# Operand tiles of a hybrid attention layer placed so that moving and stationary rows lie at equal bytes modulo 512

## The chip, the core and the metric

The kernel runs on one core of one Trainium2 chip. The metric is the device time of one execution in microseconds (us), the median of several executions. A core has a matrix engine (PE, with weight loads shown apart as PEld), a vector engine (DVE), a scalar engine (ACT), a third elementwise engine (POOL), and a queue engine (SP) that issues the DMAs. A matmul here is a pair of instructions: a weight load that puts a block of 128 rows by 128 columns of one operand (the stationary one) into the array, and a matmul that streams the rows of the other operand (the moving one) through it. Both operands are read from on-chip memory, where each of the 128 partitions holds a row of bytes; "lies at byte b modulo 512" below always means the start of an operand within such a row.

## What is computed

One decoder layer on 16 meta tokens and 1024 input tokens, 1024 wide. Cut to what matters:

```
a    = rmsnorm(concat(meta, x), ln_mix_pre)
proj = a @ w_in                                  # 3584 columns
y    = concat(diff_attention(proj), hgrn2(proj)) # 4 heads of each kind
h    = concat(meta, x) + rmsnorm(y @ w_out, ln_mix_post)
a    = rmsnorm(h, ln_ffn_pre)
u    = causal_conv3(a @ w_up) + conv_b           # 2 x 2816 columns
gate, up = split(u)
out  = h + rmsnorm((gelu(gate) * up) @ w_down, ln_ffn_post)   # meta rows dropped
```

All inputs and the output are float32.

## The kernel before

To keep float32 accuracy, each large product is done in a rounded float32 type: an operand is split into a high part (`hi`, a rounding) and a low part (`lo`, the rest), and a product is the sum of three matmuls, hi by hi, hi by lo and lo by hi. `split` makes the high part on ACT and the low part on DVE or POOL. The matmuls run in four stages, one after the other, on PE in an order that is fixed by hand (PE is the only engine whose order is the program's own; the order on the others is made by a scheduler).

1. **Projections** (to about 507 us, `proj_step`, lines 234 to 238, and line 886). The weights `wh`, `wl` are stationary; the moving rows are the normalised input, transposed, in the tiles `ahi` and `alo`: 8 blocks (index k) of 1040 columns each. Tokens go in three groups, of 272, 384 and 384 columns. Between these matmuls the small ones of the attention heads and of the HGRN heads are placed.
2. **Output projection** (about 507 to 640 us, `out_part`, lines 1012 to 1016). Here blocks of mixed heads (`mp`, in the slots X1, X2 and mp) are stationary and the split rows of `w_out` (`woh`, `wol`, 512 columns) are moving. Each 128-row block k of `w_out` comes by a DMA into a raw tile `wor` (three buffers in turn), then ACT casts `woh` and DVE or POOL makes `wol`. `out_first` uses blocks k = 0, 1, then 2, 3, then 4 to 6 for the first two token blocks, interleaved with the last HGRN head.
3. **Up projection** (about 640 to 1087 us, `unit`, lines 1378 to 1380). Each of 22 column tiles (`ft`) is done by a seven-product scheme (Strassen-Winograd) for two halves of the tokens: half p = 0 with 258 columns and p = 1 with 256. The products are j = 0 to 6, and each is 12 matmuls: 4 blocks k by three. The moving operands `t{p}_j` are split once and stay; the weights `uh`, `ul` change with each product. On PE the order within an `ft` is j = 0 for p = 0, j = 0 for p = 1, j = 1 for p = 0, and so on: 14 runs of 12 matmuls. 21 of the 22 column tiles go this way; the first is done plainly (lines 1359 to 1361).
4. **Down projection** (about 1087 to 1305 us, `mms`, lines 1536 to 1538). Blocks `gh`, `gl` are stationary, the split weights `wh`, `wl` (512 columns) are moving: 7 products by 11 blocks by 4 row blocks by 3, 924 matmuls.

Where a tile lies follows from the pools: they are stacked, and within a pool tiles lie one behind another. Most weights (`wh`, `wl`) are in a pool of their own that starts from the other end of the memory. `m0` is a constant tile of which 46 columns are used.

Of the kernel before, what the change touches and what calls it, by code (L numbers as in the profile page):

```python
# [9 lines left out]
F32 = mybir.dt.float32  # L10
F32R = mybir.dt.float32r
# [6 lines left out]
P = 128  # L18
META = 16
SEQ = 1024  # L20
L = META + SEQ
D = 1024
KD = D // P
# [3 lines left out]
NBLK = 9  # L27
# [4 lines left out]
WN = [258, 256]  # L32
# [53 lines left out]
def layer_kernel(ctx: ExitStack, tc: tile.TileContext, x, meta, table, lbl, gpre, gpost, win,  # L86
# [25 lines left out]
    def const(shape, name, dt=F32):  # L112
        return cp.tile(shape, dt, tag=name, name=name)
# [12 lines left out]
    nlam = const([P, 1], "nlam")  # L126
    cwt = const([P, 2 * NF, 3], "cwt")
    cbt = const([P, 2 * NF], "cbt")
    m0 = const([P, 152], "m0", F32R)[:, :46]
    G.memset(m0.bitcast(F32), 0.0)  # L130
    m0_7 = const([P, 2, 1, 2], "m0_7", F32R)

# [33 lines left out]

    mx_cm, mxp = pool("mix", 1)

    def long_tile(name):
        return mxp.tile([P, 8, WN[0]], F32, tag="X0", name=name).rearrange("p a c -> p (a c)")  # L170

    def parts_tile(name):
        return mxp.tile([P, 2, 384], F32R, tag="ms", name=f"ms{name}", bufs=2)
# [4 lines left out]
            SY.dma_start(msc[b0:b1, :, l, P * k:P * k + P].rearrange("b p c -> p b c"),  # L178
                         m[:, l, off:off + P * n].bitcast(F32).rearrange("p (b c) -> p b c", c=P))

    ws_cm, wsp = pool("wdsums", 6)
    at_cm, atp = pool("at", 1)
    ahi = atp.tile([P, KD, L], F32R, tag="ahi", name="ahi")
    alo = atp.tile([P, KD, L], F32R, tag="alo", name="alo")

    last_load, lows = [], []

# [59 lines left out]
    xts, xss = {}, {}  # L247

    def spare_tile(tag):
        return mxp.tile([P, 8, WN[0]], F32, tag=tag, name=f"{tag}_in").rearrange("p a c -> p (a c)")  # L250

    def load_x(i, where=None):
        xts[i] = zp.tile([P, D], F32, tag="xt", name=f"xt{i}", bufs=3) if where is None else where
# [719 lines left out]
            interleave(dense(tiles_a, None, wd_sums), [hgrn_head(t_h)] + carried(), FH, 1500)  # L973

    close(at_cm)
    wo_cm, wop = pool("wo", 7)
    y_cm, yp = pool("y0", 1)
    ml_cm, mlp = pool("mixload", 1)
    y0 = yp.tile([P, NBLK, 512], F32, tag="y0", name="y0")
    ssy = yp.tile([P, NBLK, 4], F32, tag="ssy", name="ssy")  # L980
    gpo0 = yp.tile([P, 512], F32, tag="gpo0", name="gpo0")
# [1 line left out]
    def load_wo(n):  # L983
        res = []
        for k in range(KD):
            raw = wp.tile([P, 512], F32, tag="wr", name=f"wor{n}_{k}", bufs=3)
            last_load.append(SY.dma_start(raw, wout[P * k: P * (k + 1), 512 * n: 512 * (n + 1)]))
            if n == 0 and k < 2:
                hi = wp.tile([P, 512], F32R, tag="wh", name=f"woh{n}_{k}", bufs=4)
                lo = wp.tile([P, 512], F32R, tag="wl", name=f"wol{n}_{k}", bufs=4)  # L990
            elif k < 5 if n == 0 else k > 5:
                hi, lo = (wsp.tile([P, 512], F32R, tag="wd", name=f"wo{x}{n}_{k}") for x in "hl")
            else:
                hi = wop.tile([P, 512], F32R, tag="woh", name=f"woh{n}_{k}")
                lo = wop.tile([P, 512], F32R, tag="wol", name=f"wol{n}_{k}")
            if n == 0:
                split(hi, lo, raw, V if k else G)
            else:
                with tc.issue_after(ends["a"].ins), tc.issue_after(ends["v"].ins):
                    split(hi, lo, raw, V if k % 2 else G, halved[0])  # L1000
            res.append((hi, lo))
        return res

    def tok(i):
        return (2, 14) if i == 0 else (P, start(i))
# [27 lines left out]
    def block_tile(n, i):  # L1033
        tag = SLOTS[n][i - 1]
        if tag == "mp":
            return mlp.tile([P, 2, KD, P], F32R, tag="mp", name=f"mp{n}_{i}")
        t = mxp.tile([P, 8, WN[0]], F32R, tag=tag, name=f"mp{n}_{i}")
        return t.rearrange("p a c -> p (a c)")[:, : 2 * KD * P].rearrange("p (l k t) -> p l k t", l=2, k=KD)

    def block_load(m, i, k0, k1):  # L1040
        SY.dma_start(m[:, :, k0:k1].bitcast(F32).rearrange("p l k t -> p l (k t)"), msc[i][:, :, P * k0:P * k1])
# [6 lines left out]
    def second_load(i):  # L1048
        blocks[i] = block_tile(1, i)
        block_load(blocks[i], i, 0, 4)  # L1050
        block_load(blocks[i], i, 4, 7 if i == 1 else 8)
# [51 lines left out]
    def ps_b(name):  # L1103
        return pp.tile([P, 512], F32, tag="b", name=name)
# [3 lines left out]
    e_cm, ep = pool("early", 1, "right")  # L1108
# [7 lines left out]
    q_cm, qp = pool("p2", 2, "right")  # L1116
# [51 lines left out]

    prep_plain()
    wo = load_wo(1)  # L1170
    m7 = ep.tile([P, 8, 2, P], F32R, tag="e1", name="m7")
    for i in range(1, NBLK):
        SY.dma_start(m7[:, i - 1].bitcast(F32), msc[i][:, :, P * (KD - 1):])
    gpo = qp.tile([P, 512], F32, tag="gpo", name="gpo", bufs=1)
# [5 lines left out]
    xhs = {}  # L1180

    def load_xh(i):
        r = tok(i)[0]
        if i:
            xhs[i] = qp.tile([P, D], F32, tag="xh", name=f"xh{i}")
        else:
            both = ep.tile([P, 2 * D], F32, tag="e0", name="xh0")
            xhs[i], xhs["sum"] = both[:, :D], both[:, D:]
        SY.dma_start(xhs[i][:r], meta[14:16, :] if i == 0 else x[P * (i - 1): P * i, :])

    def post(i, py, free=None):
# [47 lines left out]
    tt = [[None] * 8 for _ in range(2)]  # L1239

    def t_tiles(p, j, where, tag):
        if len(tag) == 1:
            both = where.tile([P, 8, WN[p]], F32R, tag=tag[0], name=f"t{p}_{j}")
            return both[:, 0:4], both[:, 4:8]
        both = where.tile([P, 8, int(tag[1])], F32R, tag=tag[0], name=f"t{p}_{j}")
        return both[:, 0:4, : WN[p]], both[:, 4:8, : WN[p]]

    def t_split(p, j, src, where, *tag):
        hi, lo = t_tiles(p, j, where, tag)
        A.copy(hi, src)  # L1250
        V.tensor_tensor(lo, src, hi.bitcast(F32), op=ALU.subtract)
        tt[p][j] = (hi, lo)

    def quarter(p, j):
        n = WN[p]
        a, c = {0: (0, 0), 7: (0, n), 4: (4, 0), 6: (4, n)}[j]
        return at2[p][:, a:a + 4, c:c + n]

    def t_sums(p, where, last):
        b11, b12, b21, b22 = (quarter(p, j) for j in (0, 7, 4, 6))  # L1260
        V.tensor_tensor(b11, b12, b11, op=ALU.subtract)
        V.tensor_tensor(b12, b22, b12, op=ALU.subtract)
        V.tensor_tensor(b22, b22, b11, op=ALU.subtract)
        t_split(p, 1, b22, where, f"t{p}_1")
        t_split(p, 2, b11, where, f"t{p}_2")
        t_split(p, 3, b12, where, f"t{p}_3")
        V.tensor_tensor(b21, b21, b22, op=ALU.subtract)
        t_split(p, 5, b21, *last)

    def run(*args):  # L1270
        for _ in out_part(*args):
            pass

    def k7(i):
        return m7[:, i - 1:i].rearrange("p b l t -> p l b t")

    for i in range(1, NBLK):
        py = ps_b(f"py1_{i}")
        if i >= 3:
            y0_gain(i)  # L1280
        if i == 1:
            load_xh(1)
            load_xh(0)
        if i + 1 < NBLK:
            second_load(i + 1)
            load_xh(i + 1)
        run(blocks[i], py, wo, range(4), True, False)
        if i == 3:
            trans(1)
        run(blocks[i], py, wo, range(4, 7 if i == 1 else 8), False, i > 1)  # L1290
        if i > 3:
            trans(i - 2)
        if i == 5:
            trans(0)
        if i == 1:
            pm = ps_b("py1_0")
            for _ in meta_part(pm, wo, True):
                pass
# [12 lines left out]
        if i == 2:  # L1311
            post(0, ysum[:, :512], ysum[:, 512:])
        if i == 5:
            t_split(0, 0, quarter(0, 0), ep, "e0")
            t_split(0, 4, quarter(0, 4), ep, "e1")
        if i == 7:
            t_split(0, 7, quarter(0, 7), mxp, "X2", WN[0])
            t_split(0, 6, quarter(0, 6), mxp, "X1", WN[0])
        if i in (2, 3):
            for p in (1 + 2 * i, 2 + 2 * i):  # L1320
                out_last(p)
    close(q_cm, ml_cm, y_cm, wo_cm, ws_cm)

    xu_cm, xup = pool("xu", 2)
    t_cm, tp = pool("tsplit", 1)

    marks = {}

# [85 lines left out]
        next(p0)  # L1414
    trans(8)
    t_split(1, 7, quarter(1, 7), tp, "t1_5")
    t_split(1, 6, quarter(1, 6), mxp, "X0", WN[0])
    t_sums(0, tp, (mxp, "X2", WN[0]))
    close(a_cms.pop())
    t2_cm, t2p = pool("tsplit2", 1)  # L1420
    p1 = plain_unit(1, ps_b)
    for j in range(4):
        prep(7 + j)
        next(p1)
    t_sums(1, t2p, (tp, "t1_5"))
    close(a_cms.pop(), b_cm)
    v_cm, cv = pool("conv", 2, "right")
    dn_cm, dn = pool("down", 4, "right")
    next(p0)
    for j in range(4, 7):  # L1430
# [257 lines left out]
```

## Time and profile before

| what | value |
|---|---|
| median of three runs | 1307.29 us (1307.03 to 1307.64) |
| the profiled execution's own time | 1307.29 us |
| its span, first to last instruction | 1305.5 us |
| mean granted PE clock | 0.998 |
| PE busy in the span | 1277.2 us (98%) |
| PE busy, 644 to 1087 us | 439.41 of 443.00 us |
| PE busy, 1087 to 1305.5 us | 208.95 of 218.50 us |

Reading aids: an instruction's duration for PE overlaps that of the next one, since matmuls are pipelined, so the pace of a stage is read from start to start, not from the mean duration. In the timeline a row has start and duration in us, engine, line, operation, tiles (written<-read), shape and how many equal ones were merged. In the table of stretches a row has the stretch, its length, and for each engine its busy time and its count of instructions.

### The profile page before, as it was taken

How to read it: one execution, taken by the hardware profiler on the slowest of the kernel's cores; microseconds unless marked ns; L12 is line 12 of the kernel's file. 1: busy time of each engine (PE TensorE's matmuls, PEld its weight loads, DVE VectorE, ACT ScalarE, POOL GpSimd, SP SyncE). 2: the span in 40 equal slices, each digit the busy share in tenths (PEclk: the TensorE clock that was granted, in tenths of full speed). 3: DMA queues.
4: the chain of work that ended last, by engine and by line, in shares of the span. 5: the costliest groups of instructions: out<-in, count | busy, mean ns of one | idle time of the engine just before them, and what ended most of it. 6: DMA issues, size and time to landing. Idle time of an engine off the chain costs nothing.

```text
span 1305.5 us, 26100 instructions
## 1 busy us (share of the span) xinstructions
PE 1277.2 (98%) x10154; PEld 1182.0 (91%) x10154; DVE 884.8 (68%) x1488; ACT 696.5 (53%) x1639; POOL 482.9 (37%) x387
## 2 busy tenths in 40 slices
PE   8999999999999999999999999999999999999997
PEld 7999999899999998767999999999999997888875
DVE  7574647465645574548997877877877767697586
ACT  8565466546644763447754444544544544454553
POOL 5231423242323310352076666566576631010121
PEclk9999999999999999999999999999999999999999
DMA  5243655183643533687222222222222137955263
GB/s 214 94 100 87 125 116 114 57 157 79 116 128 69 122 109 109 224 270 261 91 75 89 82 74 73 90 75 81 90 74 81 57 122 268 318 188 168 82 210 121
DMA packets 116418, 165.04 MB, mean 126 GB/s; under 512 B 10099, under 2 KB 57523, under 8 KB 116294
## 3 DMA queue, kind: packets, MB, share of 16 engines
q1 hardware_dynamic: 93062, 151.84, 35.6%
q0 software_dynamic: 23232, 11.54, 7.5%
q8 instruction: 80, 1.31, 0.4%
q14 instruction: 44, 0.36, 0.1%
HBM read 134.24 MB, written 52.17 MB: 143 GB/s over the span
## 4 chain that ended last, share of the span: by engine, by line
PE 81%; DVE 6%; DMA 4%; ACT 4%; issue 2%; SPq 0%; POOL 0%; DVEq 0%; ACTq 0%; POOLq 0%
PE pd L1537 5%; PE pd L1536 5%; PE pd L1538 5%; PE pb L1378 4%; PE pb L1380 4%; PE pb L1379 4%; PE pa L1378 3%; PE pa L1380 3%; PE pa L1379 3%; PE pc L1378 3%; PE pc L1379 3%; PE pc L1380 3%; PE pa L732 3%; PE pi_hf L234 1%; DMA ra<-in_wup_dram 1%
## 5 line engine op out<-in xcount | busy, mean ns | idle before, releaser
L1378 PE MATMUL pb<-t,uh 128*128 128x258 f32 x504 | 142.3, 282 | 2.5 <-DVE u L53 2.5
L1379 PE MATMUL pb<-t,uh 128*128 128x258 f32 x504 | 141.6, 281 | 0.0
L1380 PE MATMUL pb<-t,ul 128*128 128x258 f32 x504 | 141.6, 281 | 0.0
L1537 PE MATMUL pd<-wl,gh 128*128 128x512 f32 x308 | 122.0, 396 | 1.1 <-DVE wl L53 1.1
L1536 PE MATMUL pd<-wh,gh 128*128 128x512 f32 x308 | 121.8, 395 | 0.1
L1538 PE MATMUL pd<-wh,gl 128*128 128x512 f32 x308 | 121.7, 395 | 0.0
L53 DVE SCALAR_TENSOR_TENSOR c<-uu,cwt,c 128x514 f32<-128x514 f32 (+1 forms) x88 | 97.2, 1104 | 19.6 <-ACT c L53 18.9
L53 POOL TENSOR_TENSOR c<-c,c 128x514 f32<-128x514 f32 (+1 forms) x44 | 63.8, 1449 | 122.4 <-ACT c L53 120.4
L1378 PEld LDWEIGHTS pb<-t,uh 128*128 128x128 f32 x504 | 95.5, 189 | 3.0 <-DVE u L53 2.9
L1379 PEld LDWEIGHTS pb<-t,uh 128*128 128x128 f32 x504 | 95.5, 189 | 0.0
L1378 PE MATMUL pa<-t,uh 128*128 128x258 f32 (+1 forms) x336 | 95.2, 283 | 0.0
L1380 PEld LDWEIGHTS pb<-t,ul 128*128 128x128 f32 x504 | 95.2, 189 | 0.0
L1380 PE MATMUL pa<-t,ul 128*128 128x258 f32 (+1 forms) x336 | 95.1, 283 | 0.0
L1379 PE MATMUL pa<-t,uh 128*128 128x258 f32 (+1 forms) x336 | 94.8, 282 | 0.0
L1378 PE MATMUL pc<-t,uh 128*128 128x258 f32 (+1 forms) x336 | 94.4, 281 | 0.0
L1379 PE MATMUL pc<-t,uh 128*128 128x258 f32 (+1 forms) x336 | 94.0, 280 | 0.0
L1380 PE MATMUL pc<-t,ul 128*128 128x258 f32 (+1 forms) x336 | 93.7, 279 | 0.0
L53 DVE SCALAR_TENSOR_TENSOR c<-ug,cwt,c 128x514 f32<-128x514 f32 (+1 forms) x88 | 88.3, 1005 | 1.4 <-ACT c L53 0.6
L53 ACT CAST uh<-ra 128x512 fp32r<-128x512 f32 x67 | 41.1, 616 | 62.2 <-PE pb L1379 41.1
L53 POOL TENSOR_TENSOR ul<-ws,uh 128x512 fp32r<-128x512 f32 x42 | 60.5, 1440 | 35.5 <-ACT uh L53 34.8
L1537 PEld LDWEIGHTS pd<-wl,gh 128*128 128x128 f32 x308 | 57.7, 187 | 16.4 <-DVE wl L53 2.6
L53 DVE TENSOR_TENSOR ul<-ra,uh 128x512 fp32r<-128x512 f32 x42 | 38.7, 921 | 49.4 <-ACT uh L53 49.4
(388 smaller groups left out, 4166.3 us busy)
## 6 DMA issues: line engine op xcount, KB each, us to landing
ra<-in_wup_dram SPq DMA_DIRECT2D x88, 256.0 KB, 2.7
mp<-msc SPq DMA_DIRECT2D x23, 512.0 KB, 5.0
tsc<-in_wdown_dram SPq DMA_DIRECT2D x44, 256.0 KB, 4.8
wi<-tsc SPq DMA_DIRECT2D x44, 256.0 KB, 2.8
gi<-gsc SPq DMA_DIRECT2D x33, 256.0 KB, 5.3
wi<-in_wdown_dram SPq DMA_DIRECT2D x33, 256.0 KB, 5.3
gsc<-c SPq DMA_DIRECT2D x22, 257.0 KB, 2.1
tsc<-in_wdown_dram POOLq DMA_DIRECT2D x22, 256.0 KB, 7.5
```

The lines of the kernel that those rows point to most:

```text
L53: ins = call(*args, **kw)
L234: T.matmul(pt, hi[:, s], ahi[:, k, t0:t1], start=(k == 0), stop=False)
L732: T.matmul(po[:, :P], w_, vn[:, j], start=(j == 0), stop=(j == i))
L1378: T.matmul(pt, hi[:, s], th[:, k], start=(first and k == 0), stop=False, skip_group_check=True)
L1379: T.matmul(pt, hi[:, s], tl[:, k], start=False, stop=False, skip_group_check=True)
L1380: T.matmul(pt, lo[:, s], th[:, k], start=False, stop=(k == 3), skip_group_check=True)
L1536: T.matmul(py, gh[:, s], wh, start=(k == 0 and pr not in (3, 7)), stop=False, skip_group_check=True)
L1537: T.matmul(py, gh[:, s], wl, start=False, stop=False, skip_group_check=True)
L1538: T.matmul(py, gl[:, s], wh, start=False, stop=(k == NH - 1), skip_group_check=True)
```

## The change

No instruction is added. Tiles are made larger, shifted or put in another order, so that for most matmuls the moving and the stationary operand start at equal bytes modulo 512. The distance (start of the moving rows less start of the next stationary rows, modulo 512 bytes), as the two programs lay them out:

| matmuls | count | distance before | distance in the change |
|---|---|---|---|
| projections, group of 272 columns | 672 | 0, 64, ... 448, one step with each k | 448 |
| projections, groups of 384 | 1344 | 0, 64, ... 448, one step with each k | 0 |
| output projection, 512 columns | 418 | mostly 192, 128 and 352, few at 64 and 256 | 0 for 366 |
| up, p = 0 (258 columns), j = 0 to 6 | 252 each | 448, 256, 320, 384, 384, 320, 256 | 384, 0, 0, 0, 448, 0, 0 |
| up, p = 1 (256 columns), j = 0 to 6 | 252 each | 256, 448, 448, 448, 256, 256, 384 | 0 for all |
| down, 512 columns | 924 | 288 | 0 |

For p = 0 the number is that of the first block; each further block adds 8, and the low part lies 32 further (in the change not for j = 3). The same holds for p = 1, j = 6 before, by its tile's row length. For the up stage and the projections the stationary rows stay where they were, at 480, and the moving ones move; in the down stage the stationary ones move.

The pool `wdsums` of six tiles, which take the split blocks k = 2 to 4 of the first half of `w_out`, was opened ahead of the pool `at` of `ahi` and `alo`; it is now opened as `wosplit` after `at` is closed, in the memory that `ahi` and `alo` leave. That moves work on DVE, ACT and SP.

```
-    m0 = const([P, 152], "m0", F32R)[:, :46]
+    m0 = const([P, 88], "m0", F32R)[:, :46]
...
+    MIX = {"X0": 2048, "X1": 2176, "X2": 2176}
+    def mix_tile(tag, dt, name):
+        return mxp.tile([P, MIX[tag]], dt, tag=tag, name=name)
...
-    ws_cm, wsp = pool("wdsums", 6)
     at_cm, atp = pool("at", 1)
-    ahi = atp.tile([P, KD, L], F32R, tag="ahi", name="ahi")
-    alo = atp.tile([P, KD, L], F32R, tag="alo", name="alo")
+    ahi, alo = (atp.tile([P, KD, P * NBLK], F32R, tag=t, name=t)[:, :, P - META:] for t in ("ahi", "alo"))
...
     close(at_cm)
+    ws_cm, wsp = pool("wosplit", 6)
     wo_cm, wop = pool("wo", 7)
+    ml_cm, mlp = pool("mixload", 1)
     y_cm, yp = pool("y0", 1)
-    ml_cm, mlp = pool("mixload", 1)
...
-    m7 = ep.tile([P, 8, 2, P], F32R, tag="e1", name="m7")
+    xh0 = ep.tile([P, 2 * D], F32, tag="e0", name="xh0")
+    m7 = ep.tile([P, 8 * WN[0]], F32R, tag="e1", name="m7")[:, 16:].rearrange("p (b l t) -> p b l t", b=8, l=2)
...
     def t_tiles(p, j, where, tag):
-        if len(tag) == 1:
-            both = where.tile([P, 8, WN[p]], F32R, tag=tag[0], name=f"t{p}_{j}")
-            return both[:, 0:4], both[:, 4:8]
-        both = where.tile([P, 8, int(tag[1])], F32R, tag=tag[0], name=f"t{p}_{j}")
-        return both[:, 0:4, : WN[p]], both[:, 4:8, : WN[p]]
+        tag, n, lo = (tag + (8 * WN[p], 4 * WN[p])[len(tag) - 1:])[:3]
+        flat = where.tile([P, n], F32R, tag=tag, name=f"t{p}_{j}")
+        return [flat[:, o:o + 4 * WN[p]].rearrange("p (a c) -> p a c", a=4) for o in (0, lo)]
...
-        t_split(p, 1, b22, where, f"t{p}_1")
-        t_split(p, 2, b11, where, f"t{p}_2")
-        t_split(p, 3, b12, where, f"t{p}_3")
+        for j, b in ((1, b22), (2, b11), (3, b12)):
+            t_split(p, j, b, where, f"t{p}_{j}", *(() if p else (2304, 1152) if j == 3 else (2176,)))
...
     t_cm, tp = pool("tsplit", 1)
+    tp.tile([P, 48], F32, tag="gap", name="gap")
...
     v_cm, cv = pool("conv", 2, "right")
+    cv.tile([P, 56], F32, tag="gap2", name="gap2", bufs=1)
```

On PE the order of instructions is the same. It differs on DVE, ACT and SP where the projections end and the output projection begins. DVE before, from the gate of the last HGRN head on (`wol_k` is the low part of block k of `w_out`, `woh_k` its high part, `wor_k` the raw block, `gate` and `hq` belong to the last HGRN head):

```order
L53 TENSOR_TENSOR gate_6154<-pi_hg_1_6161,sg_1_6222 128x384
L53 TENSOR_SCALAR sg_2_6253<-sg_2_6253 128x384
L53 TENSOR_TENSOR wol_5_6311<-wor_5_6308,woh_5_6310 128x512
L53 TENSOR_TENSOR wol_6_6317<-wor_6_6314,woh_6_6316 128x512
L53 TENSOR_TENSOR gate_6154<-pi_hg_2_6228,sg_2_6253 128x384
L53 TENSOR_TENSOR wol_7_6323<-wor_7_6320,woh_7_6322 128x512
L53 TENSOR_TENSOR hq_5424<-hq_5424,f_5421 128x1040
```

And DVE in the change, at the same place:

```order
L53 TENSOR_TENSOR gate_6151<-pi_hg_1_6158,sg_1_6219 128x384
L53 TENSOR_SCALAR sg_2_6250<-sg_2_6250 128x384
L53 TENSOR_TENSOR wol_2_6293<-wor_2_6290,woh_2_6292 128x512
L53 TENSOR_TENSOR wol_3_6299<-wor_3_6296,woh_3_6298 128x512
L53 TENSOR_TENSOR gate_6151<-pi_hg_2_6225,sg_2_6250 128x384
L53 TENSOR_TENSOR wol_4_6305<-wor_4_6302,woh_4_6304 128x512
L53 TENSOR_TENSOR wol_5_6311<-wor_5_6308,woh_5_6310 128x512
L53 TENSOR_TENSOR hq_5421<-hq_5421,f_5418 128x1040
L53 TENSOR_TENSOR wol_6_6317<-wor_6_6314,woh_6_6316 128x512
L53 TENSOR_TENSOR wol_7_6323<-wor_7_6320,woh_7_6322 128x512
```

Blocks 2, 3 and 4, which stood some forty rows earlier, now stand where 5, 6 and 7 did, and 6 and 7 come behind `hq`. SP's queue before, at the loads of these blocks (`msc` is the store of mixed heads, `gpo` a gain row, `mp_3` the third token block of mixed heads):

```order
L987 DMA wor_2_6290<-in_wout_dram 128x512
L987 DMA wor_3_6296<-in_wout_dram 128x512
L987 DMA wor_4_6302<-in_wout_dram 128x512
L987 DMA wor_5_6308<-in_wout_dram 128x512
L178 DMA msc<-msa_5_6037 128x3x128 x2
L987 DMA wor_6_6314<-in_wout_dram 128x512
L987 DMA wor_7_6320<-in_wout_dram 128x512
L1058 DMA gpo_6271<-in_gpost_dram 128x512
L1041 DMA mp_3_6335<-msc 128x2x512
L1041 DMA mp_3_6335<-msc 128x2x384
```

And in the change:

```order
L991 DMA wor_2_6290<-in_wout_dram 128x512
L183 DMA msc<-msa_5_6034 128x3x128 x2
L991 DMA wor_3_6296<-in_wout_dram 128x512
L991 DMA wor_4_6302<-in_wout_dram 128x512
L1061 DMA gpo_6271<-in_gpost_dram 128x512
L1044 DMA mp_3_6335<-msc 128x2x512
L991 DMA wor_5_6308<-in_wout_dram 128x512
L991 DMA wor_6_6314<-in_wout_dram 128x512
L991 DMA wor_7_6320<-in_wout_dram 128x512
L1044 DMA mp_3_6335<-msc 128x2x384
```

The loads of blocks 5 to 7 moved behind the gain row and the first half of `mp_3`; the raw tile that each takes is free when the low part of block 2, 3 or 4 is made.

More of the change, by code (lines that the diff above doesn't have):

```diff
@@ L167, in layer_kernel @@
     mx_cm, mxp = pool("mix", 1)
+    MIX = {"X0": 2048, "X1": 2176, "X2": 2176}
+    def mix_tile(tag, dt, name):
+        return mxp.tile([P, MIX[tag]], dt, tag=tag, name=name)
     def long_tile(name):
-        return mxp.tile([P, 8, WN[0]], F32, tag="X0", name=name).rearrange("p a c -> p (a c)")
+        return mix_tile("X0", F32, name)
     def parts_tile(name):
@@ L249, in spare_tile @@
     def spare_tile(tag):
-        return mxp.tile([P, 8, WN[0]], F32, tag=tag, name=f"{tag}_in").rearrange("p a c -> p (a c)")
+        return mix_tile(tag, F32, f"{tag}_in")
     def load_x(i, where=None):
@@ L1036, in block_tile @@
             return mlp.tile([P, 2, KD, P], F32R, tag="mp", name=f"mp{n}_{i}")
-        t = mxp.tile([P, 8, WN[0]], F32R, tag=tag, name=f"mp{n}_{i}")
-        return t.rearrange("p a c -> p (a c)")[:, : 2 * KD * P].rearrange("p (l k t) -> p l k t", l=2, k=KD)
+        return mix_tile(tag, F32R, f"mp{n}_{i}")[:, : 2 * KD * P].rearrange("p (l k t) -> p l k t", l=2, k=KD)
     def block_load(m, i, k0, k1):
@@ L1186, in load_xh @@
         else:
-            both = ep.tile([P, 2 * D], F32, tag="e0", name="xh0")
-            xhs[i], xhs["sum"] = both[:, :D], both[:, D:]
+            xhs[i], xhs["sum"] = xh0[:, :D], xh0[:, D:]
         SY.dma_start(xhs[i][:r], meta[14:16, :] if i == 0 else x[P * (i - 1): P * i, :])
@@ L1316, in layer_kernel @@
         if i == 7:
-            t_split(0, 7, quarter(0, 7), mxp, "X2", WN[0])
-            t_split(0, 6, quarter(0, 6), mxp, "X1", WN[0])
+            t_split(0, 7, quarter(0, 7), mxp, "X2", MIX["X2"])
+            t_split(0, 6, quarter(0, 6), mxp, "X1", MIX["X1"])
         if i in (2, 3):
@@ L1321, in layer_kernel @@
                 out_last(p)
-    close(q_cm, ml_cm, y_cm, wo_cm, ws_cm)
+    close(q_cm, y_cm, ml_cm, wo_cm, ws_cm)
     xu_cm, xup = pool("xu", 2)
     t_cm, tp = pool("tsplit", 1)
+    tp.tile([P, 48], F32, tag="gap", name="gap")
     marks = {}
@@ L1416, in layer_kernel @@
     t_split(1, 7, quarter(1, 7), tp, "t1_5")
-    t_split(1, 6, quarter(1, 6), mxp, "X0", WN[0])
-    t_sums(0, tp, (mxp, "X2", WN[0]))
+    t_split(1, 6, quarter(1, 6), mxp, "X0")
+    t_sums(0, tp, (mxp, "X2", MIX["X2"]))
     close(a_cms.pop())
```

## The prediction

> **What bounds the kernel now.** I read the page first: the span, each engine's busy time, the chain of waits.
>
> ```profile
> span 1305.5 us, 26100 instructions
> PE 1277.2 (98%) x10154; PEld 1182.0 (91%) x10154; DVE 884.8 (68%) x1488; ACT 696.5 (53%) x1639; POOL 482.9 (37%) x387
> PE 81%; DVE 6%; DMA 4%; ACT 4%; issue 2%; SPq 0%; POOL 0%; DVEq 0%; ACTq 0%; POOLq 0%
> ```
>
> PE is busy for 98% of the span and carries 81% of the chain. Nothing is added to it or taken from it, so the time can move in two ways only: the pace at which the same 10154 matmuls start, and new waits. The profiled execution took 1307.29 us, which is also the median; 1.8 us lie outside its span. I add my terms to 1307.3. What a measurement of this kernel can tell from no change is about 0.2%, 2.6 us: below 1304.7 is faster, above 1309.9 slower.
>
> For the pace I read PE's timeline in the up stage, at the first matmul of each run of twelve. It is one column tile, j = 0 of p = 1 first; rows of p = 1 (256 columns) and p = 0 (258) alternate.
>
> ```profile
> 840.00 0.28 PE L1378 MATMUL pa<-t,uh 128*128 128x256 f32 x1
> 841.44 0.28 PE L1378 MATMUL pb<-t,uh 128*128 128x258 f32 x1
> 842.88 0.28 PE L1378 MATMUL pb<-t,uh 128*128 128x256 f32 x1
> 844.29 0.28 PE L1378 MATMUL pc<-t,uh 128*128 128x258 f32 x1
> 845.71 0.28 PE L1378 MATMUL pc<-t,uh 128*128 128x256 f32 x1
> 847.07 0.29 PE L1378 MATMUL pb<-t,uh 128*128 128x258 f32 x1
> 848.52 0.28 PE L1378 MATMUL pb<-t,uh 128*128 128x256 f32 x1
> 849.90 0.29 PE L1378 MATMUL pa<-t,uh 128*128 128x258 f32 x1
> 851.35 0.28 PE L1378 MATMUL pa<-t,uh 128*128 128x256 f32 x1
> 852.78 0.28 PE L1378 MATMUL pb<-t,uh 128*128 128x258 f32 x1
> 854.20 0.28 PE L1378 MATMUL pb<-t,uh 128*128 128x256 f32 x1
> 855.63 0.28 PE L1378 MATMUL pc<-t,uh 128*128 128x258 f32 x1
> 857.07 0.28 PE L1378 MATMUL pc<-t,uh 128*128 128x256 f32 x1
> 858.50 0.28 PE L1378 MATMUL pa<-t,uh 128*128 128x258 f32 x1
> 859.94 0.28 PE L1378 MATMUL pa<-t,uh 128*128 128x256 f32 x1
> ```
>
> From start to start the seven p = 1 runs take 1.44, 1.41, 1.36, 1.38, 1.43, 1.43, 1.43, together 9.88 us. Beside them I put the distances of the change's table: 256, 448, 448, 448, 256, 256, 384. So twelve equal matmuls cost 1.43 to 1.44 at a distance of 256 and 1.36 to 1.41 at 448. Distance matters, and so does the state in which a run begins, since 448 gives three values. The p = 0 runs, from j = 1 on and j = 0 last, take 1.44, 1.42, 1.45, 1.45, 1.42, 1.44, 1.44, together 10.06, at 256, 320, 384, 384, 320, 256, 448. The column tile lasts 19.94 us.
>
> **What distance 0 is worth.** The up stage never has it. The projections do, where the distance grows by 64 with each block of three matmuls; here are blocks 0, 1, 4, 5 and the end of the eighth step (the timeline, first matmul of each).
>
> ```profile
> 252.70 0.34 PE L234 MATMUL pi_hg<-ahi,wh_hg 128*128 128x384 f32 x1
> 253.23 0.33 PE L234 MATMUL pi_hg<-ahi,wh_hg 128*128 128x384 f32 x1
> ...
> 254.80 0.33 PE L234 MATMUL pi_hg<-ahi,wh_hg 128*128 128x384 f32 x1
> 255.32 0.34 PE L234 MATMUL pi_hg<-ahi,wh_hg 128*128 128x384 f32 x1
> ...
> 256.38 0.34 PE L234 MATMUL pi_hg<-ahi,wh_hg 128*128 128x384 f32 x1
> ```
>
> Three matmuls take 0.53 us at distance 0, 0.52 at 256, and (256.38 - 252.70) / 7 = 0.526 on average. Zero is not better than the rest, and within the 10 ns of the rows it does as 256 does. I take that for the forecast: the pattern repeats after 256 bytes, and equal bytes are the slow case of the up stage.
>
> **Up, +4.1.** In the change all p = 1 runs are at 0. At 1.43 to 1.44 each they take 10.01 to 10.08, which is 0.13 to 0.20 more than 9.88. For p = 0 five runs are at 0 (1.44 each), one at 384 (1.45), one at 448 (1.44): 10.09, 0.03 more. The sum is 0.16 to 0.23 for a column tile, middle 0.195, and 21 of the 22 go this way: 3.4 to 4.8, I take 4.1. The other end is that 0 is the free case that 256 is not. The best run (1.36) stands for it: 7 x 1.36 = 9.52, and 258/256 of it, 9.59, for p = 0. That saves 0.36 + 0.47 = 0.83 a tile, 17 us in all.
>
> **Down, -2.9.** Here the view is the table of stretches.
>
> ```profile
> core 0: us, PE busy (x) PEld busy (x) DVE busy (x) ACT busy (x) POOL busy (x), PEclk, DMA share, GB/s
> 1094.00:1242.00 148.00, 148.00 (x635) 118.75 (x635) 109.66 (x165) 74.45 (x146) 12.84 (x8) 1.00 0.62 206
> ```
>
> PE never idles, at a granted clock of 1.00, so one matmul costs 148 / 635 = 0.2331 us, at distance 288 throughout. The nearest rows for 512 columns at another distance are in the output projection, a change of place within the same loop (timeline again).
>
> ```profile
> 507.26 0.39 PE L1012 MATMUL py<-woh,mp 128*128 128x512 f32 x1
> ...
> 508.39 0.39 PE L1016 MATMUL py<-woh,mp 128*128 128x512 f32 x1
> 508.62 0.40 PE L1012 MATMUL py<-woh,mp 128*128 128x512 f32 x1
> ...
> 511.64 0.39 PE L1014 MATMUL py<-wol,mp 128*128 128x512 f32 x1
> ...
> 552.96 0.39 PE L1012 MATMUL py<-woh,mp 128*128 128x512 f32 x1
> ...
> 553.88 0.39 PE L1014 MATMUL py<-wol,mp 128*128 128x512 f32 x1
> ```
>
> From 507.26 to 508.39 the distance is 256: five steps of 0.226, the fastest pace of this shape. From 508.62 to 511.64 it is 192: thirteen steps of 0.2323. From 552.96 to 553.88 it is 256 again: four steps of 0.230. The same distance gives two paces, as 448 does in the up stage; and short runs need not show the pace that a long one settles at. The bounds are therefore 0.226 (924 x 0.0071 = 6.6 saved) and no gain. I take 0.230, the slower of the two rows: 924 x 0.0031 = 2.9 saved.
>
> **Output projection, -0.8.** 366 matmuls come to 0; from 0.2323 to 0.230 that is 0.8, bounds 0 and 366 x 0.0063 = 2.3.
>
> **Projections, 0.** The groups of 384 columns go from the mean of eight distances to 0, 0.526 against 0.53 by the rows above: within a row's rounding. The best pace of the up stage, 1.36 / 12 for 256 columns, gives 0.170 for 384, so that 1344 x (0.526 / 3 - 0.170) = 7 us could be saved, and about 3 on the 672 of 272 columns at the same excess; on the other side 1344 x 0.004 / 3 = 1.8 could be lost.
>
> **The hand-over, +2.0.** The pool `wosplit` now lies in the memory of `ahi` and `alo`, so the splits of blocks 2 to 4 wait for the last projection matmul (507.1). What that drags along shows in the timeline on PE, ACT, DVE and SP's queue, and in the landing times of the DMA issues of 505 to 520 and of the whole page.
>
> ```profile
> 507.85 0.61 ACT L53 CAST woh<-wor 128x512 fp32r<-128x512 f32 x1
> 508.49 0.69 DVE L53 TENSOR_TENSOR wol<-wor,woh 128x512 fp32r<-128x512 f32 x1
> 509.59 1.03 SPq L987 DMA_DIRECT2D wor<-in_wout_dram  x2
> wor<-in_wout_dram SPq DMA_DIRECT2D x3, 256.0 KB, 5.7
> ra<-in_wup_dram SPq DMA_DIRECT2D x88, 256.0 KB, 2.7
> 512.80 1.24 DVE L53 TENSOR_TENSOR hq<-hq,f 128x1040 f32<-128x1040 f32 x1 [1.50 <-PE pd L436]
> 513.91 0.39 PE L1014 MATMUL py<-wol,mp 128*128 128x512 f32 x1
> 514.61 0.39 PE L1014 MATMUL py<-wol,mp 128*128 128x512 f32 x1
> ```
>
> The raw tiles of blocks 5 to 7 are now those of 2 to 4 and come free with the low parts, on DVE from 507.4 on. Before, the blocks after 4 could be loaded ahead; now the loads stand in SP's queue behind the gain row and the first half of `mp_3`, so they go at about 509.6 at the earliest. They land 2.7 (a load of equal size, whole page) to 5.7 us later (median of the window): 512.3 to 515.3. A cast (0.61) and a low part (0.69) make block 5's low part ready at 513.6 to 516.6, against a use at 513.91. Then DVE does `hq` (1.24) and block 6 (0.69): 515.5 to 518.5, against 514.61. Late are 0.9 to 3.9, and PE has nothing else in its order; queued behind on DVE is block 7, needed 0.7 after block 6 and ready as long after it. I take 2.0. Nothing later hides it, since PE bounds the rest.
>
> The other edits (a smaller `m0`, gaps, `xh0` opened earlier, two pools swapped) issue nothing and only place tiles.
>
> **Sum:** 1307.3 + 4.1 - 2.9 - 0.8 + 0 + 2.0 = 1309.7 us. Its own range, with the hand-over's bounds and up's, is 1307 to 1312.
>
> **Rivals.**
>
> *Long runs settle slow.* The up stage's 1.44 at 256 is a settled excess that stays through twelve matmuls, and down has runs of 924. If 0 holds the excess there too, down and output projection gain nothing: 1307.3 + 4.1 + 2.0 = 1313.4, slower. For it: the pace at 256 is already 0.230 in the second stretch. Against it: 0.226 in the first.
>
> *The pace of 507.26 is the lasting one.* Down saves 6.6 and the output projection 2.3: 1307.3 + 4.1 - 6.6 - 2.3 + 2.0 = 1304.5, at the edge of faster. For it: five steps in succession. Against it: the stretch at 552.96.
>
> *Equal bytes free every stage.* 0 and 256 would differ, and all runs go at their best: 1307.3 - 17.3 - 6.6 - 2.3 - 10 + 2.0 = 1273. Against it: the 0.53 at 252.70, at exactly this distance.
>
> *Placement is worth nothing* and only the hand-over is left: 1307.3 + 2.0 = 1309.3. Against it: 1.36 and 1.44 for equal instructions. The Trainium skill speaks for it ("SBUF — State Buffer", section "Who interferes with whom"): it gives PE two read ports, one for the moving operand and one for the weight load, independent of each other, so that where one lies could not disturb the other. By that rule the sum would lose its first four terms; the trace does not agree, since the runs of the up stage differ by 0.08 us at the same shapes, with PE waiting for no other engine.
>
> **How the numbers follow.** Chances: my sum 33%, slow settling 32%, the fast pace in down 20%, all stages free 8%, placement worth nothing 7%. The range takes in the first three and the last with their bounds, 1302 to 1315, and leaves out the free case and some tails. Faster: the free case, half of the fast pace and a little of the first, 22%. Within 0.2%: half of my sum, most of placement worth nothing, the rest of the fast pace, 30%. Slower: the rest, 48%.
>
> **What would show it.** A column tile of the up stage lasts 20.13 instead of 19.94, with all seven p = 1 runs at 1.43 to 1.44; the same stretch of the down stage holds about 643 matmuls (148 / 0.230) instead of 635, or 655 at 0.226; the triples of the projections stay at 0.53; and between 513 and 519 PE waits about 2 us for `wol` on DVE. The forecast is wrong if the p = 1 runs fall to 1.36 with all at distance 0, if the pace in down rises above 0.2331, or if the loads of blocks 5 to 7 land before 512.

## The result and the profile after

| | before | the change |
|---|---|---|
| median of 14 runs each | 1307.07 us | 1308.16 us (1307.37 to 1313.38) |
| ratio to before, 95% interval | | 1.0014 (1.0004 to 1.0024) |
| the profiled execution's own time | 1307.29 us | 1310.98 us |
| its span | 1305.5 us | 1309.2 us |

The change costs about 0.14%, with an interval that lies just above 1; that is below the 0.2% that the prediction took as the least it could tell from no change. The profiled execution is one of the longer ones, 2.8 us above the median; part of what it has more is told with the hand-over below. Three moves that nearly cancel lie behind the small number. The page of the change first: span, busy time, chain.

```profile
span 1309.2 us, 26099 instructions
PE 1275.9 (97%) x10154; PEld 1186.7 (91%) x10154; DVE 887.3 (68%) x1488; ACT 697.0 (53%) x1639; POOL 480.8 (37%) x387
PE 82%; DVE 6%; ACT 4%; DMA 4%; issue 2%; SPq 0%; POOL 0%; DVEq 0%; ACTq 0%
```

It reads as before: the same 10154 matmuls, PE busy nearly all the time. So I compared the start of the n-th matmul in the two traces, which works because PE's order is the same. The difference after less before, in us, at the ends of the stages:

| up to | difference |
|---|---|
| last matmuls ahead of the first new wait (514 us) | +0.2 |
| behind the new waits (522 us) | +4.3 |
| start of the up stage | +4.5 |
| end of the up stage | +8.4 |
| last matmul | +3.5 |

So the hand-over costs 4.1, the up stage 3.9, and the down stage gives back 4.9. The up stage, on PE's timeline of the change (first matmul of some runs of twelve; `t` is 256 wide in p = 1, 258 in p = 0):

```profile
845.97 0.28 PE L1379 MATMUL pa<-t,uh 128*128 128x256 f32 x1
847.39 0.28 PE L1379 MATMUL pb<-t,uh 128*128 128x258 f32 x1
848.83 0.28 PE L1379 MATMUL pb<-t,uh 128*128 128x256 f32 x1
850.26 0.28 PE L1379 MATMUL pc<-t,uh 128*128 128x258 f32 x1
851.70 0.28 PE L1379 MATMUL pc<-t,uh 128*128 128x256 f32 x1
853.14 0.28 PE L1379 MATMUL pb<-t,uh 128*128 128x258 f32 x1
...
866.11 0.28 PE L1379 MATMUL pa<-t,uh 128*128 128x256 f32 x1
```

The p = 1 run that took 1.36 before (j = 2, from 845.71) takes 853.14 - 851.70 = 1.44 now, and the others 1.42 and 1.43: all stand at the slow value. The column tile lasts 866.11 - 845.97 = 20.14 us. The down stage, in the same stretch as before:

```profile
1094.00:1242.00 148.00, 147.95 (x650) 121.49 (x650) 110.12 (x168) 73.31 (x139) 9.84 (x8) 1.00 0.67 219
```

650 matmuls in place of 635, so 148 / 650 = 0.2277 us each. And the hand-over, on ACT, DVE and SP's queue, then what PE waited for from 513 to 520:

```profile
509.48 2.44 SPq L991 DMA_DIRECT2D wor<-in_wout_dram  x3
508.75 0.69 DVE L53 TENSOR_TENSOR wol<-wor,woh 128x512 fp32r<-128x512 f32 x1
515.76 1.96 ACT L53 CAST woh<-wor 128x512 fp32r<-128x512 f32 x3 [5.05 <-DMA wor<-in_wout_dram]
516.41 0.69 DVE L53 TENSOR_TENSOR wol<-wor,woh 128x512 fp32r<-128x512 f32 x1 [4.85 <-ACT woh L53]
517.02 1.23 DVE L53 TENSOR_TENSOR hq<-hq,f 128x1040 f32<-128x1040 f32 x1
518.17 0.69 DVE L53 TENSOR_TENSOR wol<-wor,woh 128x512 fp32r<-128x512 f32 x1
PE py L1016 <- ACT woh L53: 1.7, 1, 1.7
PE py L1018 <- DVE wol L53: 0.2, 1, 0.2
```

The chain can be followed row by row. DVE makes the low part of block 2 from 508.75 to 509.44; 0.04 later SP issues the load into the raw tile that this frees; ACT's cast of block 5 begins when it lands, at 515.76, 6.3 after the issue; PE waits 1.66 us for that cast. Then come block 5's low part, `hq`, and block 6's low part, which is done at 518.86. The matmul that uses it, before and in the change:

```profile
515.56 0.48 PE L1014 MATMUL py<-wol,mp 128*128 128x512 f32 x1
518.91 0.80 PE L1018 MATMUL py<-wol,mp 128*128 128x512 f32 x1
```

It starts 3.35 us later than before, where the matmuls at 514 us started 0.2 later: the chain costs 3.1 of the 4.1. The other 1.0 comes behind it, under a lower granted clock (stretches of the same trace: length, PE busy and count, granted clock, DMA share, GB/s):

```profile
517.00:518.00 1.00, 0.84 (x3) 0.92 0.04 14
518.00:520.00 2.00, 1.97 (x7) 0.50 0.50 141
520.00:521.00 1.00, 1.00 (x9) 0.50 0.89 272
521.00:522.00 1.00, 1.00 (x67) 0.87 1.01 254
```

By these rows the clock was at one half for some 3.4 us; in the kernel before it is 1.00 from 513 to 520.

### The profile page after: what moved, and what is told of

It reads as the page before. It is cut to its first block, busy times and chain, and to the rows that moved or that the text cites. A ratio compares the mean times of both kernels' runs of the same rounds, so it can differ in the third digit from the quotient of the medians.

```text
span 1309.2 us, 26099 instructions
## 1 busy us (share of the span) xinstructions
PE 1275.9 (97%) x10154; PEld 1186.7 (91%) x10154; DVE 887.3 (68%) x1488; ACT 697.0 (53%) x1639; POOL 480.8 (37%) x387
## 4 chain that ended last, share of the span: by engine, by line
PE 82%; DVE 6%; ACT 4%; DMA 4%; issue 2%; SPq 0%; POOL 0%; DVEq 0%; ACTq 0%
PE pd L1539 5%; PE pd L1540 5%; PE pd L1538 5%; PE pb L1379 5%; PE pb L1380 4%; PE pb L1381 4%; PE pa L735 3%; PE pa L1379 3%; PE pa L1381 3%; PE pa L1380 3%; PE pc L1379 3%; PE pc L1380 3%; PE pc L1381 3%; PE pt L711 1%; PE S L655 1%
## 5 line engine op out<-in xcount | busy, mean ns | idle before, releaser
L53 POOL TENSOR_TENSOR c<-c,c 128x514 f32<-128x514 f32 (+1 forms) x44 | 63.8, 1450 | 122.6 <-ACT c L53 119.2
```

The source lines that it names most:

```text
L53: ins = call(*args, **kw)
```

## The experiments

**The pace by distance, measured alone.**

```diff
+    for n in (512, 256, 258, 272, 384):
+        for r in range(0, 512, 16):
+            a = 120 + r // 4
+            for _ in range(3):
+                py = banks[g % 4][:, :n]
+                g += 1
+                for q in range(12):
+                    T.matmul(py, w, mv[:, a:a + n], start=(q == 0), stop=(q == 11))
```

> This kernel computes nothing of the layer: it writes zeros to the output and runs 5760 matmuls of one shape after another, 36 for each distance from 0 to 496 in steps of 16, at 512, 256, 258, 272 and 384 columns. Theory (the pace is set by the distance modulo 256 and the width): at 256 columns the steps at a distance and at that distance plus 256 agree within 1 ns, 120 at 0 and 256 and 113 to 118 at 192 and 448; at 512 columns 227 at 0 and 233 at 32 (that is 288). Rival (equal bytes modulo 512 are a case of their own): 0 and 256 differ at 512 columns. Second rival (the pace follows from the neighbouring engines' traffic, not from the distance): with the other engines idle all distances run at one pace, 113 at 256 columns and 227 at 512.

Four rows of its timeline (start, time from the first start to the last end, count): 512 columns at distance 0 and 288, 256 columns at 0 and 112.

```profile
7.45 5.83 PE L114 MATMUL b<-mv,st 128*128 128x512 f32 x25
157.63 6.00 PE L114 MATMUL b<-mv,st 128*128 128x512 f32 x25
273.31 3.28 PE L114 MATMUL b<-mv,st 128*128 128x256 f32 x26
303.18 3.11 PE L114 MATMUL b<-mv,st 128*128 128x256 f32 x26
```

One matmul lasts 0.39 or 0.28, so a step is (5.83 - 0.39) / 24 = 0.2267 against (6.00 - 0.39) / 24 = 0.2338, and (3.28 - 0.28) / 25 = 0.120 against (3.11 - 0.28) / 25 = 0.113. PE alone is at work here, so neighbouring traffic is not what makes the difference. All settled paces, in ns, as the mean of the last twelve of 36 steps from the start times in the trace:

| distance mod 256 | 0 | 16 | 32 | 48 | 64 | 80 | 96 | 112 | 128 | 144 | 160 | 176 | 192 | 208 | 224 | 240 |
|---|---|---|---|---|---|---|---|---|---|---|---|---|---|---|---|---|
| 256 columns | 120.0 | 118.8 | 116.7 | 118.3 | 117.8 | 120.0 | 120.0 | 113.3 | 118.8 | 118.3 | 117.1 | 119.4 | 113.3 | 118.7 | 117.9 | 117.4 |
| 258 | 120.0 | 116.7 | 120.0 | 120.0 | 118.6 | 120.2 | 120.0 | 120.0 | 120.0 | 120.0 | 119.7 | 120.0 | 120.8 | 121.7 | 120.3 | 119.2 |
| 272 | 126.7 | 124.6 | 125.7 | 125.0 | 126.7 | 125.0 | 126.7 | 123.3 | 126.7 | 124.4 | 123.3 | 123.3 | 123.3 | 126.7 | 126.7 | 125.0 |
| 384 | 173.3 | 175.5 | 173.3 | 175.0 | 173.3 | 173.3 | 176.7 | 173.3 | 175.8 | 174.7 | 176.7 | 176.4 | 176.7 | 176.7 | 173.3 | 180.0 |
| 512 | 226.7 | 231.7 | 233.3 | 233.3 | 228.9 | 231.1 | 233.3 | 231.1 | 231.7 | 233.3 | 234.2 | 233.3 | 233.3 | 234.8 | 233.3 | 226.7 |

The same distance plus 256 gives the same mean within 0.4 ns at every place of the table. So equal bytes modulo 512 are no case of their own, and what distance is good depends on the width: 0 is among the best for 512 columns and among the worst for 256. At 512 columns and 256 bytes the first twelve steps average 229.9 and the last twelve 226.7. That fits the two paces the prediction found at one distance in the output projection, if its slower row was a short run that had not settled. In this map only the moving rows change place, so by itself it cannot tell the distance from the moving rows' own place. The down stage can: there the stationary rows were moved, and its two paces, 233.3 and 226.9 ns from start to start, are those of the map at 288 and at 0 within 0.2 ns.

**Another distance with the same remainder.**

```diff
-    m0 = const([P, 88], "m0", F32R)[:, :46]
+    m0 = const([P, 152], "m0", F32R)[:, :46]
-    cv.tile([P, 56], F32, tag="gap2", name="gap2", bufs=1)
+    cv.tile([P, 120], F32, tag="gap2", name="gap2", bufs=1)
```

(To make room, `t0_3` is laid out as `t0_1` is, its low part 32 bytes further.)

> The change with moving and stationary rows 256 bytes apart modulo 512 in the projections, the up and the down stage, in place of 0. Theory (the pattern repeats after 256 bytes): no difference, 1308.2 us within 1.5, with a column tile of the up stage at 20.14 us and the down stage at 0.2277 a matmul as in the change. Rival (equal bytes modulo 512 matter as such): the down stage loses its gain of 4 to 5 us, 1312.5 or more.

1309.31 us, ratio to before 1.001 (1.000 to 1.0019), against 1.0014 for the change. From start to end of the up stage it loses 3.9 us on the kernel before, and the down stage gives back 5.1; in the stretch from 1094 to 1242 us it has 651 matmuls. At these distances 256 bytes more make no difference in the kernel either.

**The down stage alone.**

```diff
     v_cm, cv = pool("conv", 2, "right")
+    cv.tile([P, 56], F32, tag="gap2", name="gap2", bufs=1)
```

(on the kernel before)

> The kernel before with the gap in the pool of the down stage alone, which brings that stage from a distance of 288 to 0. Theory: 924 matmuls at 0.2277 in place of 0.2331, 4 to 5 us less, 1302.5 us. Rival (the gain in the trace of the change came from loads that stood earlier, since everything before was later by 8 us): 1306 to 1307.

1302.49 us, ratio 0.9958 (0.9945 to 0.9972), 650 matmuls in the stretch again. One unused tile of 224 bytes, which moves `gh` and `gl` and leaves `wh` and `wl` where they are, is worth 4.8 us by the medians, and the gain needs nothing of the rest of the change.

**The hand-over taken out, and alone.** The first puts the pool back where it was in the change (for which `ahi` and `alo` need their old layout, and X1 and X2 are 2112 long in place of 2176), the second moves it in the kernel before.

```diff
+    ws_cm, wsp = pool("wosplit", 6)
     at_cm, atp = pool("at", 1)
-    ahi, alo = (atp.tile([P, KD, P * NBLK], F32R, tag=t, name=t)[:, :, P - META:] for t in ("ahi", "alo"))
+    ahi, alo = (atp.tile([P, KD, L], F32R, tag=t, name=t) for t in ("ahi", "alo"))
...
     close(at_cm)
-    ws_cm, wsp = pool("wosplit", 6)
```

> The change with the pool of the split blocks opened ahead of ahi and alo again, and so with the projections' old layout. Theory: the wait at the hand-over, about 4 us in the trace, goes and nothing else moves: 1304.2 us, slightly faster than before. Rival: PE would have met the same wait a little later, at a store or load of mixed heads, so that 2 us or less come back: 1306 to 1308.

1306.73 us, ratio 0.9994 (0.9985 to 1.0003). In its trace the wait is gone: from the last projection matmul to the start of the up stage it moves by nothing against the kernel before (0.9 to 0.9 us), then up +3.9 and down -5.4. Against the change it saves 0.2% by the two ratios to before, 2.6 us (1.4 by the bare medians), and I had expected 4, from the one trace with the half clock in it. The time falls in the range that the rival gave, 1306 to 1308, but not for its reason: no such wait comes back later in the trace.

```diff
-    ws_cm, wsp = pool("wdsums", 6)
     at_cm, atp = pool("at", 1)
...
     close(at_cm)
+    ws_cm, wsp = pool("wosplit", 6)
     wo_cm, wop = pool("wo", 7)
```

> The kernel before with the pool of the split blocks opened where ahi and alo are closed, and nothing else: all distances are those of before. Theory (a wait on PE at the hand-over, 2.4 and 4.1 us in two traces, and nothing gives it back): 1307.1 + 2.5 = 1309.6 us, between 1308.8 and 1311. Rival (what the split blocks lose is made good by the memory that opens earlier, or was due to the new layout of ahi and alo): 1307.1 within 0.7.

1310.06 us (1307.45 to 1311.90), ratio 1.0017 (1.0007 to 1.0026): 0.17% of 1307.8, 2.2 us slower. PE's waits in its trace from 513 to 520 us:

```profile
PE py L1012 <- ACT woh L53: 1.2, 1, 1.2
PE py L1014 <- DVE wol L53: 0.7, 2, 0.5
518.00:520.00 2.00, 1.55 (x42) 1.00 0.43 146
```

The same waits on the same blocks, 1.9 us, with the clock at 1.00 (last row): the half clock of the change's profiled execution is not a fixed part of the price. The matmul with block 6's low part is 2.7 us late here, and 2.4 in the trace of the run 256 bytes apart, with the first load landing 5.9 and 5.6 us after its issue. Up to the start of the up stage further waits move this again: against the kernel before, the stretch from the last projection matmul to there is longer by 4.2 us in the change's trace, 3.0 in that of the run 256 bytes apart and 4.3 here. One trace gives the price to about a microsecond; the ratios are the better measure. The distances are all those of the kernel before, so the layout of `ahi` and `alo` has no part in it.

**Can the up stage be had without the loss?** The map offers 112 for 256 columns. A second one ran pairs of runs as the up stage does, to find a partner for p = 0.

```diff
+    def twelve(pt, hi, lo, step, n):
+        for k in range(4):
+            for q, a in enumerate((hi, lo, hi)):
+                o = 120 + (a + k * step) // 4
+                T.matmul(pt[:, :n], w, mv[:, o:o + n], start=(k + q == 0), stop=(k == 3 and q == 2))
...
+                    for _ in range(2):
+                        twelve(banks[g % 4], r0, r0 + lo, step, 258)
+                        twelve(banks[(g + 1) % 4], r1, r1, 0, 256)
+                        g += 2
```

> This kernel computes nothing of the layer: zeros are written to the output, and 8448 matmuls run as the up stage has them, twelve of 258 columns (four blocks of high, low, high) and then twelve of 256, with the 256 ones at a distance of 112 and the 258 ones at distances that start from 0 to 248, with the low part at several offsets, and with 8 or 0 bytes from block to block. Theory (distance, width and the state left by the run before set the pace, and nothing else): every run of 256 columns settles at 113.3 within its twelve, so 1.36 to 1.37 us against 1.433 at distance 0; the 258 ones spread from about 1.39 to 1.46, and the settings that the change has (0 with the low part at 32) give 1.44. Rival (112 was fast only because 96 came before it): the 256 ones stay at 1.40 or more behind most settings.

The rival was right in the main: of 175 settings at 112 that can be timed, the second p = 1 run took under 1.37 us in 11 and 1.38 to 1.43 in 157. A run of twelve does not come to the pace of a long one by itself; which p = 0 run stands before it decides. The best with the up stage's own steps (8 bytes a block, low part at 32) was a start at 8: 1.434 + 1.360 = 2.794 us. It was built into the kernel, with the pool where it was before the change and the gaps set to suit:

```diff
+    AT = {(0, 1): 42, (0, 2): 42, (0, 3): 42, (0, 5): 18, (0, 6): 18, (1, 6): 44, (0, 0): 2, (0, 4): 2, (1, 0): 4, (1, 1): 4, (1, 2): 4, (1, 3): 4, (1, 4): 4, (1, 5): 4}
...
+        n = tag[1] if len(tag) > 1 else 2056 if (p, j) == (1, 3) else 2112
+        flat = where.tile([P, n], F32R, tag=tag[0], name=f"t{p}_{j}")
+        a, w = AT.get((p, j), 0), 4 * WN[p]
+        return [flat[:, o:o + w].rearrange("p (a c) -> p a c", a=4) for o in (a, a + w)]
```

> The kernel with the old pool order at the hand-over (as in pool_back) and with the up stage's tiles at other distances: 112 modulo 256 for all p = 1 runs, 8 rising by 8 with each block (low part 32 further) for all p = 0 runs, down and output projection at 0 as in the change. Theory (the distances alone set the pace, so the pair measured by itself carries over): a pair of runs takes 1.434 + 1.360 = 2.794 us in place of 2.874, a column tile 19.56 in place of 20.14, and 21 of them save 12 us against pool_back: 1306.7 - 12 = 1295 us. Rival (with DVE, ACT and POOL busy beside PE the fast state does not last, as one of three runs at 448 in the kernel before went at 1.415): the p = 1 runs come to 1.39 to 1.41, a column tile to 19.8, and the time to 1299 or more.

1303.65 us, ratio 0.9969 (0.9958 to 0.9979). A pair of its timeline, with the start of the next:

```profile
850.41 0.28 PE L1382 MATMUL pa<-t,uh 128*128 128x258 f32 x1
851.86 0.28 PE L1382 MATMUL pa<-t,uh 128*128 128x256 f32 x1
853.27 0.28 PE L1382 MATMUL pb<-t,uh 128*128 128x258 f32 x1
```

The pair takes 1.45 and 1.41, and does so for all seven j and every column tile from the third on. The pair measured alone did not carry over: same distances, another steady sequence, 2.85 in place of 2.79. That is the number of the rival, but its reason (the busy engines beside PE) was not tested.

**Is it the state, or the weights' places?** One more map laid the weights as the kernel does and passed through the settings upwards and downwards; and one kernel took the pair that the kernel before itself had run fastest, j = 2.

> This kernel computes nothing of the layer: zeros are written to the output, and pairs of runs go as in the up stage, now with weights that lie as there (high, high, low, four blocks), three equal pairs for each start distance of the 258 columns from 0 to 248 (low part 32 further, 8 more with each block), once upwards and once downwards, with the 256 columns at 112 and then at 192. Theory (a setting has more than one lasting state, and the state before chooses): the third pair of some settings differs between the upward and the downward pass, and 8 with 112 gives 2.794 in one and 2.853 in the other. Rival (the weights' places beyond 256 bytes count): both passes give 2.853 at 8 with 112, and agree everywhere.

At 112 both passes agree, and 8 gives 2.794 in both; at 192 some settings settle differently from the two sides (a start at 24: 2.840 upwards, 2.800 downwards). Other settings alternate between two values from pair to pair (a start of 176 with 112: 2.874, 2.812, 2.874). So one setting can have more than one state that holds over the three pairs, which supports the first part of the theory; but the 2.853 of the kernel at 8 with 112 appeared in neither pass. The weights' places, as far as this map copies them, are not it. What in the kernel chooses another state stays open: the maps run with the other engines idle and on zeros, so neither the neighbours nor the data are excluded.

```diff
-    AT = {(0, 1): 42, (0, 2): 42, (0, 3): 42, (0, 5): 18, (0, 6): 18, (1, 6): 44, (0, 0): 2, (0, 4): 2, (1, 0): 4, (1, 1): 4, (1, 2): 4, (1, 3): 4, (1, 4): 4, (1, 5): 4}
+    AT = {(0, 1): 32, (0, 2): 32, (0, 3): 32, (0, 5): 32, (0, 6): 32, (0, 0): 16, (0, 4): 16}
...
-    tp.tile([P, 24], F32, tag="gap", name="gap")
+    tp.tile([P, 48], F32, tag="gap", name="gap")
```

> As the run named best, with all p = 0 runs at 64 (modulo 256, 8 more with each block, low part 32 further) and all p = 1 runs at 192: the pair that took 1.417 + 1.359 = 2.776 as j = 2 in the kernel before. Theory (distances set the pace, state and all): if the state that j = 2 had there lasts, a column tile takes 19.43, 0.50 less than before, and the time is 1303.65 - 21 x (19.97 - 19.43) = 1292.3 us. Rival (the pair falls into another lasting state once it follows itself): a column tile of 19.8 to 20.0 and 1300 to 1304 us.

1298.70 us, ratio 0.9931 (0.9918 to 0.9945): faster than both kernels, 9.3 us below its runs of before by the medians. Its timeline:

```profile
850.12 0.28 PE L1382 MATMUL pb<-t,uh 128*128 128x258 f32 x1
851.55 0.28 PE L1382 MATMUL pb<-t,uh 128*128 128x256 f32 x1
852.91 0.28 PE L1382 MATMUL pc<-t,uh 128*128 128x258 f32 x1
```

The p = 1 run takes 1.36 and stays there in all seven j; the p = 0 run takes 1.43 where 1.417 was hoped for. A column tile lasts 19.55 us, where the theory said 19.43 and the rival 19.8 or more. The pair is 2.793 us here, was 2.776 as j = 2 in the kernel before, and is 2.814 in the last map: three values for one setting. The stage gains 5.4 us on the kernel before, not 21 x 0.38 = 8.0, in part because three of the 20 tiles that can be timed take 20.2. There PE waits for DVE to read the bank `pb` (j = 1, `u<-pb,x`) before j = 3 can write it again. From 660 to 1080 us, first the kernel before and then this one (total, times, longest):

```profile
PE pb L1378 <- DVE u L53: 2.5, 2, 1.4
```

```profile
PE pb L1382 <- DVE u L53: 3.7, 5, 1.5
```

One of the three new waits, on DVE and on PE:

```profile
745.53 0.68 DVE L53 TENSOR_TENSOR ul<-ws,uh 128x512 fp32r<-128x512 f32 x1
746.13 0.74 DVE L53 TENSOR_TENSOR u<-pb,x 128x258 f32<-128x258 f32 x2
746.60 0.39 PE L1382 MATMUL pb<-t,uh 128*128 128x258 f32 x1 [0.31 <-DVE u L53]
```

DVE comes to the read late, behind the low part of other weights. A still faster pace may meet more such waits; no run shows it.

## Why the prediction was right

It gave 1309.7 us, with 1307 to 1312 for its own sum and 1302 to 1315 over the rivals, and 1308.16 was measured. The mechanism was right: slower in the up stage, faster in the down stage, a new wait between. That the total came so near is in part luck, for errors of its terms went against each other: the down stage gained about 2 us more than was said, the output projection's 0.8 did not reach the stage's end, and the hand-over cost a little more. Of the three outcomes it held "slower" the likeliest, at 48%, and "within 0.2%", which came, had 30%. By its steps:

- **What bounds the kernel.** Right: PE's pace and the new waits at the hand-over explain the difference.
- **Up, +4.1.** Right in mechanism and size: 20.14 us a column tile where 20.13 was said, 3.9 us over the stage in the traces of three kernels with these distances or those 256 further. The reading that 0 does as 256 does, made from rows with 10 ns of rounding, holds to within 0.4 ns when measured alone.
- **Down, -2.9.** Right in direction, too small: 4.9 to 5.4 in four traces. The step that was mis-sized is the choice of 0.230, the slower of the two rows. The faster row, five steps at 0.226, has the lasting pace (226.9 ns from start to start in the stage, 226.7 in the map); the slower one looks like a run that had not yet settled, as the map's first twelve steps at 229.9. The prediction drew the opposite from short runs.
- **Output projection, -0.8.** The pace came further than was said, from 232.4 to 228.5 ns from start to start (mean over some 370 steps in each trace) where 0.230 was taken; over 366 matmuls that is 1.4 us. The stage's end does not show it. In the change's trace the difference to the kernel before falls from 4.5 us at 548 to 3.1 just ahead of 612, and is back at 4.3 there: PE waits 1.3 us for DVE (line 1233, `pa<-ident,a`), which it did not do before at this matmul. At the load of mixed heads (`mp<-msc`) it waits 1.7 us, 1.3 before. What the pace gained was given back at these two waits.
- **Projections, 0.** Right: +0.3 us at their end. From start to start 384 columns went from 174.6 to 174.8 ns, 272 columns from 125.5 to 123.8. The map alone has 173.3 for 384 columns at 0; why the kernel stays above it was not looked into.
- **The hand-over, +2.0.** The chain was right: the raw tile freed by block 2's low part, the load at 509.48 where 509.6 was said, block 5's cast, `hq` ahead of block 6. By the ratios the price is 2.2 us alone, and 2.6 between the change and the kernel without it; at the matmul with block 6's low part the three traces have 2.4, 2.7 and 3.1. Two readings were off, in opposite directions. The first load took 5.6 to 6.3 us to land, where 5.7 was the upper bound. And the uses were read one block early: 513.91 and 514.61 are the low parts of blocks 4 and 5, and block 6's is used at 515.56, so that the prediction's own bounds should have given 0 to 2.9 late in place of 0.9 to 3.9. PE's longest wait was for block 5's cast on ACT, not for a low part on DVE. The half clock that followed in one trace was not thought of.
- **Rivals.** Slow settling is out for 512 columns, though 256 columns do settle at their slowest pace at 0. The fast pace in down is what happened; its sum of 1304.5 was not reached, because of the 6.6 and 2.3 us that it counted for down and output projection 4.9 to 5.4 and nothing arrived at the stages' ends. That equal bytes free every stage is out by the map and by the up stage's 20.14. That placement is worth nothing is out by one unused tile worth 4.8 us; the Trainium skill's statement that PE's two read ports are independent of each other ("SBUF — State Buffer", section "Who interferes with whom") does not agree with 113.3 against 120.0 ns for the same instruction on an otherwise idle core.

## What to carry to other kernels

On a stage bound by the matrix engine, read the pace from start to start by shape and compare it with the best run of the same shape: measured alone, 3 to 6% lay between the best and the worst place of the moving rows against the weights that load beneath them, and in the kernel 2.7% of the down stage's pace. No distance was the best for all the widths measured, so each stage is set by itself. The one setting taken from a pair measured alone lost its gain in the kernel, and the one taken from a fast run of the kernel's own kept most of it; that is one case of each. A layout that has to move a buffer to make room is paid for where that buffer comes free: here 2.2 to 2.6 us, about half of what the down stage gained.

## What the hardware showed that was not expected

- The pace depends on the distance modulo 256 and on the width, in steady sequences that repeat to 1 ns: 113.3 to 120.0 ns at 256 columns, 226.7 to 234.8 at 512, with PE alone at work. Why a given width favours a given distance was not found.
- Some settings have two states that hold over three pairs, chosen by what ran before (2.840 or 2.800 us a pair at a start of 24 with 192).
- After a wait of 1.66 us and one of 0.23, PE's granted clock stood at 0.50 for some 3.4 us in one execution, with no drop in two others that waited 1.6 and 1.9 us in three pieces each, 0.9 and 1.2 the longest. The Trainium skill ("TensorE: Matmul & The Clock Gate", section "What's actually happening") has the clock halved after an idle window of about 3.4 us; the time at half clock is of that size here, and the wait ahead of it is only half as long. In the trace with the drop the mean granted clock is 0.996, in those of the other kernels 0.997 or 0.998. Over all executions it is 0.996 in 3 of 14 of the change, 3 of 11 of the kernel 256 bytes apart and 1 of 11 of the move alone, in none of the 31 of the four kernels without the move, and in 1 of 59 of the kernel before. So the drop seems to come with this wait in some executions; it does not explain all of the scatter, for the move alone took 1310.98 us at 0.997.
